# Weight splits between the steps of a pair's chain, and bias blocks in every second group, in a two-layer decoder trunk

## The chip, the cores and the metric

The kernel runs on one core of a Trainium2 chip. The time is the device time of one execution in microseconds; the kernel before takes 565.17 us (median of three runs, 564.53 to 566.84).

## What is computed

A trunk of two layers over 256 tokens with 1024 features, float32. Layer 0 mixes tokens by latent attention, layer 1 by block attention with a T5 bias; each is followed by an MLP with squared ReLU. The change touches the two MLPs alone.

```python
def sq_relu_mlp(h, w_in, w_out):        # w_in 1024 x 4096, w_out 4096 x 1024
    a = jax.nn.relu(h @ w_in)
    return (a * a) @ w_out

for i in range(DEPTH):                  # DEPTH = 2
    ...                                 # token mixer i, added to x
    h = rms_norm(x, mlp_norm[i])
    x = x + sq_relu_mlp(h, mlp_w_in[i], mlp_w_out[i])
```

In layer 1 each logit of the attention gets `rel_bias_table.T[h, t5_bucket(pos_q - pos_k)]` added. The kernel builds that bias (8 heads, 384 columns) during the MLP of layer 0.

## The kernel before

Everything is kept transposed: features on the 128 partitions, tokens along the row. To reach float32's accuracy with the fast matmul type, every operand is split into a high part (rounded) and a low part (the rest), and each product is three matmuls: high x high, low x high, high x low (`mm3`, 256 columns each). The row scale of the norm is not applied to h; it multiplies the result afterwards (`scale`).

**Weights** come in 185 units of 128 x 1024 numbers (512 KB), in the order of their use. SP's queue loads a unit into one of four `raw` buffers (`load_raw`), the scalar engine (ACT) rounds it into `wh` (`hi`, L169), the vector engine (DVE) subtracts to get `wl` (`lo`, L178). `wh` and `wl` have seven buffers each; `hi` does nothing when its unit is more than seven ahead of the last unit given as done (`done`). A raw buffer is free again after `lo`. `fill` (L181) does one low split, then one high split, so the low part of a unit is made a call later than its high part.

**The MLP** (`mlp`) has two halves r = 0, 1. In each half come eight *pairs* j (`first`): 256 columns of w_in, two units, 48 matmuls, and then a *chain* that makes `a`: relu (ACT, L922), square (DVE, L924), high part (ACT, L929), low part (DVE, L930). In layer 1's second half a multiplication by `scale` stands after the square. Then come eight *groups* d of w_out, two units and 48 matmuls each, numbered 8 to 15 behind the pairs; they read `a` of all eight pairs, the last pair's at the 43rd to 48th matmul. A group ends with y = psum x scale (DVE, L965) and x + y (POOL, L967). In the second half of layer 0 `finish0` goes on: x + y (POOL, L1030; DVE for the last), `make_h_filled` with hTh (ACT, L603), one `fill`, and hTl (DVE, L605), which is the input of layer 1's projections; after every second group ACT squares x for the next norm (L293) and POOL sums it (L295).

**The bias** is made in 12 blocks (`BiasBlock`), each in two places of layer 0's MLP. `steps`: the DVE compares positions, 128 x 1024, into `st` (L1006; two buffers). One place later `sums`: eight bf16 matmuls of 96 columns with `st` as weights, put into TensorE's row behind the 43rd matmul of the pair or group; and `add`: six DVE additions (L1023). `run_fillers` calls `steps` and `add` of a place. After matmuls of another type the first matmul of the next pair or group is made 258 columns wide (`wider`, L103).

Each engine works through its own instructions in the order in which the code issues them; the order of the lines in `mlp` is the order on the engines.

Of the kernel before, what the change touches and what calls it, by code (L numbers as in the profile page):

```python
# [25 lines left out]
KD = D // P  # L26
# [34 lines left out]
def trunk(ctx: ExitStack, tc: tile.TileContext, A, out):  # L61
# [119 lines left out]
    def fill(n=1):  # L181
        lo(n)
        hi(n)

    def unit(i):
        while len(his) <= i:
# [705 lines left out]
    def mlp(l, base, fillers, inside, finish):  # L892

        with tc.tile_pool(name=f"mlp{l}", bufs=1) as pool:
# [10 lines left out]
            def first(b, r, j, split_k, between=None):  # L905
                u = [unit(b + 2 * j + i) for i in range(2)]
                p = [ps() for _ in range(2 if split_k else 1)]
                o = [p[f][:, :S] if split_k else p[0][:, f * S:(f + 1) * S] for f in range(2)]
                for f, k in [(f, k) for k in range(KD) for f in range(2)] if split_k else \
                        [(f, k) for f in range(2) for k in range(KD)]:  # L910
                    c = (k % 4) * 256 + f * P
                    wide = None
                    if k == f == 0 and not moved[0]:
                        wide = wider(p[f], hTh)
                    mm3(o[f], part(u[k // 4], slice(c, c + P)), hT(k), k == 0, k == KD - 1, wide,
                        between if (f, k) == (1, KD - 2) else None)
                fill(2)
                run_fillers(r, j)
                for f, n in ((0, 1), (1, 1)) if split_k else ((0, 2),):
                    src = o[f] if split_k else p[0]  # L920
                    rl = t2(n * S)
                    nc.scalar.activation(rl, src, AF.Relu)  # L922
                    sq = t2(n * S)
                    nc.vector.scalar_tensor_tensor(sq, src, 0.0, rl, op0=OP.max, op1=OP.mult)  # L924
                    if l == 1 and r == NR - 1:
                        sq3 = sq.rearrange("p (a b) -> p a b", b=S)
                        nc.vector.tensor_mul(sq3, sq3, scale[:, None, :].to_broadcast([P, n, S]))
                    ah, al = (i[:, 2 * j + f:2 * j + f + n].rearrange("p a b -> p (a b)") for i in a)
                    nc.scalar.copy(ah, sq)  # L929
                    nc.vector.tensor_sub(al, sq, f32(ah))  # L930
                done(b + 2 * j + 1)

            for r in range(NR):
                b = base + r * (2 * NPAIR + 2 * KD)
                for j in range(NPAIR):
                    between = inside.get((r, j))
                    if r == 0 and j == 6:
                        pb = ps()
                        between = other_type(1, lambda: mm(pb[:, :S], ones, s, True, True))
                    first(b, r, j, r == 0 and j == 0, between)  # L940
                    if r == 0 and 1 <= j < 5:
                        sums.add(j - 1)
                    if r == 0 and j == 5:
                        s = sums.total()
                    if r == 0 and j == NPAIR - 1:
                        nc.vector.tensor_scalar(scale, pb[:, :S], 1.0 / D, EPS, op0=OP.mult, op1=OP.add)
                        nc.vector.reciprocal(scale, scale)
                b += 2 * NPAIR
                for d in range(KD):
                    bank = ps()  # L950
                    o = bank[:, :S]
                    for f in range(2 * NPAIR):
                        u = unit(b + 2 * d + f // 8)
                        c = (f % 8) * P
                        mm3(o, part(u, slice(c, c + P)), (a[0][:, f], a[1][:, f]), f == 0, f == 2 * NPAIR - 1,
                            wider(bank, a[0]) if f == 0 and not moved[0] else None,
                            inside.get((r, NPAIR + d)) if f == 2 * NPAIR - 2 else None)
                        if f == 7:
                            fill()
                            done(b + 2 * d)  # L960
                    fill()
                    run_fillers(r, NPAIR + d)
                    if l == 0 or r < NR - 1:
                        y = t2(S)
                        nc.vector.tensor_tensor(y, o, scale, op=OP.mult)  # L965
                        if r < NR - 1:
                            nc.gpsimd.tensor_add(x[:, d], y, x[:, d])  # L967
                            o = None
                        else:
                            o = y  # L970
                    if o is not None:
                        finish(d, o)
                    done(b + 2 * d + 1)
# [69 lines left out]
    inside = {}  # L1043
    fillers = [((0, 1), table_loads), ((0, 5), bias_tables)]
    for i, b in enumerate(blocks):
        r, j = (0, NPAIR + i) if i < KD else (1, (1, 4, 8, 10)[i - KD])
        place = (r, j + 1) if j + 1 < 2 * NPAIR else (r + 1, 0)
        fillers += [((r, j), b.steps), (place, b.add)]
        inside[place] = other_type(0, b.sums)
# [154 lines left out]
```

## Time and profile before

| | us |
|---|---|
| median of three runs | 565.17 |
| the profiled execution | 564.64 |
| its span | 562.5 |
| TensorE busy | 556.4 (99%) |
| DVE busy | 407.4 (72%) |
| ACT busy | 307.1 (55%) |
| POOL busy | 108.6 (19%) |

The page gives each engine's busy time. A timeline gives an engine's instructions with their start, and the idle time before them with what ended it; instructions of one kind in a row are one line with a count, whose time is from the first start to the last end. Ends of matmuls are modelled, and they overlap, so the pace of TensorE is read from starts, or from how many of them a stretch holds. PEld is its weight load. A wait can show there as a few tenths of a microsecond between starts.

### The profile page before, as it was taken

The numbers are of one execution on the slowest core, as the hardware profiler recorded it, in microseconds if no ns is written. First come the engines' busy times: TensorE is split into PE (matmuls) and PEld (weight loads), VectorE is DVE, ScalarE is ACT, GpSimd is POOL, SyncE is SP. The second block draws the span as 40 slices with busy tenths as digits, with TensorE's granted clock in tenths as the row PEclk, the third lists the DMA queues.
The fourth block names the chain that finished last, engine by engine and source line by source line (L and its number), as shares of the span: only waits on it lengthen the run. The fifth ranks groups of instructions, "written<-read, shape, count | busy, mean of one in ns | idle before, by whom it ended". The sixth has DMA issues, their size and how long they took to land.

```text
span 562.5 us, 10755 instructions
## 1 busy us (share of the span) xinstructions
PE 556.4 (99%) x4346; PEld 530.0 (94%) x4346; DVE 407.4 (72%) x654; ACT 307.1 (55%) x495; POOL 108.6 (19%) x105
## 2 busy tenths in 40 slices
PE   8999999999999999999999999999999999999997
PEld 6878999999999999999988888999999999999997
DVE  5997778587999987786658466777787665777641
ACT  5989676665343455543555465747655533555420
POOL 4892100041132200024324100000140232000100
PEclk9999999999999999999999999999999999999999
DMA  8833445655556656575665554444465766455830
GB/s 302 291 125 114 149 130 169 188 167 182 176 167 188 182 158 215 168 231 184 212 188 152 193 177 128 137 150 153 152 185 178 257 193 196 150 180 195 258 127 29
DMA packets 29185, 99.56 MB, mean 177 GB/s; under 512 B 3824, under 2 KB 4720, under 8 KB 29136
## 3 DMA queue, kind: packets, MB, share of 16 engines
q1 hardware_dynamic: 28656, 97.94, 54.4%
q0 software_dynamic: 336, 0.92, 0.4%
q8 instruction: 34, 0.56, 0.4%
q14 instruction: 15, 0.12, 0.1%
q10 hardware_dynamic: 144, 0.02, 0.0%
HBM read 97.82 MB, written 1.05 MB: 176 GB/s over the span
## 4 chain that ended last, share of the span: by engine, by line
PE 96%; DMA 2%; SPq 1%; issue 0%; DVE 0%; ACT 0%
PE ps L85 93%; PE ps L366 1%; DMA xs<-in_x_tok 1%; DMA win<-in_w_in 1%; PE ps L590 1%; SPq L158 0%; SPq L224 0%; PE ps L506 0%; DVE wl L178 0%; ACT wh L169 0%; DVE t L1039 0%; ACT sqj L471 0%; PE ps L873 0%
## 5 line engine op out<-in xcount | busy, mean ns | idle before, releaser
L169 ACT CAST wh<-raw 128x1024 fp32r<-128x1024 f32 x177 | 183.6, 1048 | 111.6 <-DMA raw<-in_w_out_mlp 56.6
L178 DVE TENSOR_TENSOR wl<-raw,wh 128x1024 fp32r<-128x1024 f32 x177 | 226.6, 1308 | 8.9 <-ACT wh L169 8.5
L85 PE MATMUL ps<-a,wh 128*128 128x256 f32 x1024 | 178.8, 278 | 0.0
L85 PEld LDWEIGHTS ps<-a,wh 128*128 128x128 f32 x1024 | 155.5, 188 | 0.4 <-DVE a L930 0.4
L85 PE MATMUL ps<-a,wl 128*128 128x256 f32 x512 | 142.9, 279 | 0.0
L85 PE MATMUL ps<-hTl,wh 128*128 128x256 f32 x512 | 141.9, 277 | 0.0
L85 PE MATMUL ps<-hTh,wl 128*128 128x256 f32 x512 | 141.8, 277 | 0.0
L85 PE MATMUL ps<-hTh,wh 128*128 128x256 f32 (+1 forms) x512 | 141.5, 276 | 0.0
L85 PEld LDWEIGHTS ps<-a,wl 128*128 128x128 f32 x512 | 96.2, 188 | 0.0
L85 PEld LDWEIGHTS ps<-hTh,wh 128*128 128x128 f32 x512 | 96.1, 188 | 0.1
L85 PEld LDWEIGHTS ps<-hTl,wh 128*128 128x128 f32 x512 | 96.1, 188 | 0.1
L85 PEld LDWEIGHTS ps<-hTh,wl 128*128 128x128 f32 x512 | 96.1, 188 | 0.0
L85 PE MATMUL ps<-aT,wh 128*128 128x256 f32 (+1 forms) x256 | 50.4, 288 | 0.0
L85 PE MATMUL ps<-wh,hTh 128*128 128x512 f32 (+2 forms) x128 | 46.2, 386 | 1.7 <-DVE wh L440 1.1
L85 PE MATMUL ps<-wl,hTh 128*128 128x512 f32 (+2 forms) x128 | 45.2, 378 | 0.1
L85 PE MATMUL ps<-wh,hTl 128*128 128x512 f32 (+2 forms) x128 | 44.8, 377 | 0.0
L967 POOL TENSOR_TENSOR x<-t,x 128x256 f32<-128x256 f32 x16 | 25.5, 1594 | 93.1 <-DVE t L965 93.1
L929 ACT CAST a<-t 128x512 fp32r<-128x512 f32 (+1 forms) x34 | 20.2, 596 | 38.3 <-DVE t L924 26.2
L85 PEld LDWEIGHTS ps<-aT,wh 128*128 128x128 f32 x256 | 40.3, 188 | 0.2
L924 DVE SCALAR_TENSOR_TENSOR t<-ps,t 128x512 f32<-128x512 f32 (+1 forms) x34 | 22.4, 658 | 24.1 <-ACT t L922 24.0
L930 DVE TENSOR_TENSOR a<-t,a 128x512 fp32r<-128x512 f32 (+1 forms) x34 | 22.5, 661 | 22.5 <-ACT a L929 22.5
L264 POOL TENSOR_TENSOR hrs<-hss,mhalf 128x4 f32<-128x4 f32 (+1 forms) x18 | 23.2, 1298 | 65.4 <-DVE hss L341 48.8
(166 smaller groups left out, 643.3 us busy)
## 6 DMA issues: line engine op xcount, KB each, us to landing
raw<-in_w_in_mlp SPq DMA_DIRECT2D x64, 512.0 KB, 4.0
raw<-in_w_out_mlp SPq DMA_DIRECT2D x64, 512.0 KB, 4.4
raw<-in_w_qkv SPq DMA_DIRECT2D x24, 512.0 KB, 4.4
raw<-in_w_u SPq DMA_DIRECT2D x8, 512.0 KB, 6.1
win<-in_w_in SPq DMA_DIRECT2D x8, 352.0 KB, 5.3
raw<-in_w_o0a SPq DMA_DIRECT2D x4, 512.0 KB, 3.9
raw<-in_w_o0b SPq DMA_DIRECT2D x4, 512.0 KB, 3.5
raw<-in_w_o1a SPq DMA_DIRECT2D x4, 512.0 KB, 4.1
```

What stands on the lines that cost most here:

```text
L85: nc.tensor.matmul(o, a, b, start=start, stop=stop)
L169: (eng.copy if eng is nc.scalar else eng.tensor_copy)(his[i][:, :w], raws[i][:, :w])
L178: eng.tensor_sub(los[i][:, :w], raws[i][:, :w], f32(his[i][:, :w]))
L264: nc.gpsimd.tensor_tensor(dst, t, mhalf[:, :n].rearrange("p (a b) -> p a b", b=t.shape[-1]) if len(t.shape) == 3 else mhalf[:, :n], op=OP.pow)
L366: nc.tensor.transpose(pt[:, i * P:(i + 1) * P], yf[:, i * P:(i + 1) * P], ident)
L590: nc.tensor.transpose(pt[:, i * P:(i + 1) * P], self.p[:, i * P:(i + 1) * P], ident)
L924: nc.vector.scalar_tensor_tensor(sq, src, 0.0, rl, op0=OP.max, op1=OP.mult)
L929: nc.scalar.copy(ah, sq)
L930: nc.vector.tensor_sub(al, sq, f32(ah))
L967: nc.gpsimd.tensor_add(x[:, d], y, x[:, d])
```

## The change

A new helper `both` makes a unit's high part and its low part right behind it. In `first`, `done` for the pair's two units comes ahead of the chain. `fill(2)` and `run_fillers` ahead of the chain are gone. For all pairs but the first of a layer and the last of each half (`beside`), one `both` stands between square and high part of `a`; after the chain come one more `both` (two for the pairs that have none inside), a further one for pairs 1 to 3, and then `run_fillers`. The groups use `both` where they used `fill`; `make_h_filled` keeps its `fill`. The steps of bias blocks 0 to 3 are put in groups 8, 10, 12, 14 of the first half, and those of blocks 4 to 11 in pairs and groups 0, 2, ... 14 of the second half; `sums` and `add` follow one place later. Before, blocks 0 to 7 had groups 8 to 15 of the first half, and the last four had pairs 1 and 4 and groups 8 and 10 of the second.

```diff
@@ -181,6 +181,12 @@
     def fill(n=1):
         lo(n)
         hi(n)
+
+    def both(n=1):
+
+        for _ in range(n):
+            hi()
+            lo()
 
     def unit(i):
         while len(his) <= i:
@@ -914,8 +920,10 @@
                         wide = wider(p[f], hTh)
                     mm3(o[f], part(u[k // 4], slice(c, c + P)), hT(k), k == 0, k == KD - 1, wide,
                         between if (f, k) == (1, KD - 2) else None)
-                fill(2)
-                run_fillers(r, j)
+                done(b + 2 * j + 1)
+
+
+                beside = not split_k and j < NPAIR - 1
                 for f, n in ((0, 1), (1, 1)) if split_k else ((0, 2),):
                     src = o[f] if split_k else p[0]
                     rl = t2(n * S)
@@ -925,10 +933,13 @@
                     if l == 1 and r == NR - 1:
                         sq3 = sq.rearrange("p (a b) -> p a b", b=S)
                         nc.vector.tensor_mul(sq3, sq3, scale[:, None, :].to_broadcast([P, n, S]))
+                    if beside:
+                        both()
                     ah, al = (i[:, 2 * j + f:2 * j + f + n].rearrange("p a b -> p (a b)") for i in a)
                     nc.scalar.copy(ah, sq)
                     nc.vector.tensor_sub(al, sq, f32(ah))
-                done(b + 2 * j + 1)
+                both((1 if beside else 2) + (1 <= j < 4))
+                run_fillers(r, j)
 
             for r in range(NR):
                 b = base + r * (2 * NPAIR + 2 * KD)
@@ -956,9 +967,9 @@
                             wider(bank, a[0]) if f == 0 and not moved[0] else None,
                             inside.get((r, NPAIR + d)) if f == 2 * NPAIR - 2 else None)
                         if f == 7:
-                            fill()
+                            both()
                             done(b + 2 * d)
-                    fill()
+                    both()
                     run_fillers(r, NPAIR + d)
                     if l == 0 or r < NR - 1:
                         y = t2(S)
@@ -1043,7 +1054,7 @@
     inside = {}
     fillers = [((0, 1), table_loads), ((0, 5), bias_tables)]
     for i, b in enumerate(blocks):
-        r, j = (0, NPAIR + i) if i < KD else (1, (1, 4, 8, 10)[i - KD])
+        r, j = (0, NPAIR + 2 * i) if i < 4 else (1, 2 * (i - 4))
         place = (r, j + 1) if j + 1 < 2 * NPAIR else (r + 1, 0)
         fillers += [((r, j), b.steps), (place, b.add)]
         inside[place] = other_type(0, b.sums)
```

How this moves instructions is seen in the engines' rows. `t` is a work buffer, `a_1321` and `a_1322` the high and low parts of `a`. First the DVE at the start of layer 0's second half. Before, from the square of pair 0 (`t_2608`) to that of pair 1 (`t_2677`):

```order
L924 SCALAR_TENSOR_TENSOR t_2608<-ps,t_2606 128x512
L930 TENSOR_TENSOR a_1322<-t_2608,a_1321 128x512
L178 TENSOR_TENSOR wl<-raw,wh 128x1024 x2
L1006 TENSOR_TENSOR st<-steps_q,steps_k 128x1024
L924 SCALAR_TENSOR_TENSOR t_2677<-ps,t_2675 128x512
L930 TENSOR_TENSOR a_1322<-t_2677,a_1321 128x512
```

After, from the square of pair 0 (`t_2538`) to that of pair 1 (`t_2617`):

```order
L932 SCALAR_TENSOR_TENSOR t_2538<-ps,t_2536 128x512
L178 TENSOR_TENSOR wl<-raw,wh 128x1024
L940 TENSOR_TENSOR a_1322<-t_2538,a_1321 128x512
L178 TENSOR_TENSOR wl<-raw,wh 128x1024
L1017 TENSOR_TENSOR st<-steps_q,steps_k 128x1024
L932 SCALAR_TENSOR_TENSOR t_2617<-ps,t_2615 128x512
L178 TENSOR_TENSOR wl<-raw,wh 128x1024
```

The two splits before `st` belonged to pair 1 and came ahead of its chain, and `st` was that of pair 1's place; now two splits and `st` of pair 0's place are behind the steps of pair 0's own chain.

ACT at the same place, before, from the relu of pair 0 to that of pair 1:

```order
L922 ACTIVATE t_2606<-ps 128x512
L929 CAST a_1321<-t_2608 128x512
L169 CAST wh<-raw 128x1024 x2
L922 ACTIVATE t_2675<-ps 128x512
L929 CAST a_1321<-t_2677 128x512
```

After:

```order
L930 ACTIVATE t_2536<-ps 128x512
L169 CAST wh<-raw 128x1024
L939 CAST a_1321<-t_2538 128x512
L169 CAST wh<-raw 128x1024
L930 ACTIVATE t_2615<-ps 128x512
```

A high split that stood behind the high part of `a` now stands ahead of it.

The DVE in the groups of layer 0's second half. Before, from y of group 9 (`t_3269`) to y of group 10 (`t_3343`):

```order
L965 TENSOR_TENSOR t_3269<-ps,scale 128x256
L178 TENSOR_TENSOR wl<-raw,wh 128x1024
L605 SCALAR_TENSOR_TENSOR hTl<-x,gains,hTh 128x256
L178 TENSOR_TENSOR wl<-raw,wh 128x1024 x2
L1006 TENSOR_TENSOR st<-steps_q,steps_k 128x1024
L965 TENSOR_TENSOR t_3343<-ps,scale 128x256
```

After, from y of group 9 (`t_3241`) to y of group 10 (`t_3311`):

```order
L976 TENSOR_TENSOR t_3241<-ps,scale 128x256
L611 SCALAR_TENSOR_TENSOR hTl<-x,gains,hTh 128x256
L178 TENSOR_TENSOR wl<-raw,wh 128x1024 x2
L1017 TENSOR_TENSOR st<-steps_q,steps_k 128x1024
L976 TENSOR_TENSOR t_3311<-ps,scale 128x256
```

No split is left between y and hTl. On ACT the two high splits of a group stand between hTh of one group and hTh of the next, before and after.

## Rows read from the trace of the kernel before

**Rows 1.** Page, parts 1 and 4: busy time and share; the chain by engine.

```profile
PE 556.4 (99%) x4346; PEld 530.0 (94%) x4346; DVE 407.4 (72%) x654; ACT 307.1 (55%) x495; POOL 108.6 (19%) x105
...
PE 96%; DMA 2%; SPq 1%; issue 0%; DVE 0%; ACT 0%
```

**Rows 2.** Stretches: us, then each engine's busy us (instructions), granted clock, DMA.

```profile
132.00:276.00 144.00, 144.00 (x1297) 143.10 (x1296) 120.29 (x181) 67.19 (x80) 25.32 (x16) 1.00 0.59 187
...
422.00:519.00 97.00, 97.00 (x858) 97.00 (x857) 67.37 (x73) 47.71 (x56) 12.30 (x8) 1.00 0.60 193
519.00:559.00 40.00, 40.00 (x342) 40.00 (x340) 17.72 (x20) 11.05 (x11) 4.03 (x7) 1.00 0.45 148
```

**Rows 3.** TensorE's timeline: start, us, engine, operation, count, idle time and its releaser.

```profile
143.04 0.30 PEld L85 LDWEIGHTS ps<-a,wh 128*128 128x128 f32 x2 [0.18 <-DVE a L930]
...
519.02 0.45 PE L85 MATMUL ps<-a,wh 128*128 128x256 f32 x2
519.31 0.28 PE L85 MATMUL ps<-a,wl 128*128 128x256 f32 x1
```

**Rows 4.** TensorE's timeline at a bias block: eight short matmuls, then the next.

```profile
201.88 0.52 PE L85 MATMUL ps<-parts,st 128*128 128x96 bf16 x8
...
202.42 0.28 PE L85 MATMUL ps<-hTl,wh 128*128 128x256 f32 x1
```

**Rows 5.** Timelines of TensorE, ACT, DVE: one pair's chain in layer 1.

```profile
393.89 0.28 PE L85 MATMUL ps<-hTh,wh 128*128 128x256 f32 x1
...
394.09 0.60 ACT L922 ACTIVATE t<-ps 128x512 f32<-128x512 f32 x1 [1.36 <-PE ps L85]
395.45 0.62 ACT L929 CAST a<-t 128x512 fp32r<-128x512 f32 x1 [0.76 <-DVE t L924]
...
394.72 0.69 DVE L924 SCALAR_TENSOR_TENSOR t<-ps,t 128x512 f32<-128x512 f32 x1 [2.30 <-ACT t L922]
396.10 0.69 DVE L930 TENSOR_TENSOR a<-t,a 128x512 fp32r<-128x512 f32 x1 [0.69 <-ACT a L929]
```

**Rows 6.** DVE's timeline, w_out groups of layer 0's second half.

```profile
249.60 2.36 DVE L178 TENSOR_TENSOR wl<-raw,wh 128x1024 fp32r<-128x1024 f32 x2
251.87 1.22 DVE L1006 TENSOR_TENSOR st<-steps_q,steps_k 128x1024 bf16<-128x1024 f32 x1
253.01 0.41 DVE L965 TENSOR_TENSOR t<-ps,scale 128x256 f32<-128x256 f32 x1
253.34 1.21 DVE L178 TENSOR_TENSOR wl<-raw,wh 128x1024 fp32r<-128x1024 f32 x1
255.73 0.48 DVE L605 SCALAR_TENSOR_TENSOR hTl<-x,gains,hTh 128x256 fp32r<-128x256 f32 x1 [1.18 <-ACT hTh L603]
256.67 1.23 DVE L178 TENSOR_TENSOR wl<-raw,wh 128x1024 fp32r<-128x1024 f32 x1 [0.45 <-ACT wh L169]
257.82 0.28 DVE L1023 TENSOR_TENSOR bias<-ps,mask 128x128 f32<-128x128 f32 x1
...
259.52 0.41 DVE L965 TENSOR_TENSOR t<-ps,scale 128x256 f32<-128x256 f32 x1
```

**Rows 7.** POOL's and ACT's timelines, same stretch: x + y, hTh, the high splits.

```profile
253.57 1.59 POOL L1030 TENSOR_TENSOR x<-t,x 128x256 f32<-128x256 f32 x1 [4.95 <-DVE t L965]
...
255.19 0.51 ACT L603 ACTIVATE hTh<-x,gains 128x256 fp32r<-128x256 f32 x1 [3.61 <-POOL x L1030]
255.61 1.99 ACT L169 CAST wh<-raw 128x1024 fp32r<-128x1024 f32 x2
```

**Rows 8.** ACT's, POOL's and DVE's timelines in a group with the norm's square.

```profile
262.10 0.62 ACT L293 ACTIVATE t<-x 128x512 f32<-128x512 f32 x1
...
262.80 1.30 POOL L295 TENSOR_TENSOR ssum<-t,t 128x512 f32<-128x512 f32 x1 [1.14 <-ACT t L293]
...
263.69 1.48 DVE L178 TENSOR_TENSOR wl<-raw,wh 128x1024 fp32r<-128x1024 f32 x1 [0.98 <-ACT wh L169]
```

**Rows 9.** DVE's timeline, the reciprocal ahead of layer 0's first w_out group.

```profile
143.36 1.75 DVE L947 RECIPROCAL scale<-scale 128x256 f32<-128x256 f32 x1
```

## The prediction

> **What bounds the kernel now.** I read the page first: TensorE is busy for 99% of the span, and the chain that ended last is 96% TensorE [rows 1]. So only two things move the end: how fast TensorE takes its matmuls, and how long it waits between them. Next the stretches. In 422 to 519 us it takes 858 matmuls in 97.0 us, 0.1132 us each; in 519 to 559 it takes 342 in 40.0 us, 0.1178 us each, at the same granted clock of 1.00 (the upper level, 2.4 GHz) [rows 2]. There are two paces, and the slow one costs 4%. The rows around the change of pace show what starts it: from 519.02 to 519.31 two matmuls take 0.29 us instead of 0.23 [rows 3]. That is the end of the first w_out group of layer 1's second half, where the last pair's `a` is read. At the same place in layer 0, at 143.04, a weight load has waited for the DVE's `a` [rows 3]. In this kernel a short wait of TensorE is therefore paid twice: once itself, and then by the slow pace until a widened matmul (258 columns, `wider`) comes, if one comes.
>
> How much is that in all? 132 to 276 us holds 1297 matmuls, 96 of them the short ones of the bias blocks. A block costs TensorE 0.43 us: from 201.88 to 202.42 is 0.54, with one long matmul of 0.11 in it [rows 4]. 144.0 - 1199 x 0.1132 - 12 x 0.43 leaves 3.1 us; about 0.3 of it is the six slow matmuls around each block, which stay. In 519 to 559 it is 40.0 - 340 x 0.1132 = 1.5 us. So **all waits and all slow pace in the two MLPs are worth 2.8 + 1.5 = 4.3 us**. That is the most the change can win there: 564.64 us (the profiled execution; span 562.5; the median of the three is 565.17) would become 560.3.
>
> **The change, part by part.**
>
> *Last pair's chain first* (relu, square, high, low, then the splits). After a pair's last matmul (next pair begins at 393.89) the relu starts 0.20 later, the square 0.83, the low part of `a` 2.2, ending at 2.9 [rows 5]. TensorE needs it at the 43rd matmul of the next group, 43 x 0.1132 = 4.87 us. This wait goes, in both layers: here the 1.5 us of layer 1 and the slow stretch behind 143.04 are won. In layer 1 nothing else is moved onto TensorE's path, since it has no bias blocks and its last add needs no `hT`.
>
> *High and low split together, between the chain's steps.* No instruction is added. Low parts come right behind high parts, six units ahead of their use; the wait at a late low part goes with the rest of the 4.3. But the chain gets longer: relu to 0.80, high split to 1.8 (two take 1.99 on ACT [rows 7]), low split 1.8 to 3.0, low part of `a` to 3.6, second low split 3.55 to 4.75. For `a` itself that does no harm, it is read much later.
>
> *The bias steps behind that chain.* This does harm. `run_fillers` moves from ahead of the chain to behind it. Before, `st` of a pair stood in the DVE's row ahead of the pair's square and needed nothing of that pair. Now it stands behind square, low split, low part, low split (front: the DVE's rows), so it cannot start before 4.7 us after the pair's end, and takes 1.22 [rows 6]: it ends at 5.9. TensorE wants it at the 43rd matmul of the next pair, 4.87 us after, and its queue stands still until then. That is a wait of 1.05 us, four times (blocks 4 to 7, in pairs 1, 3, 5, 7 of the second half). Behind pair 1 a third split (1.14) and the adds (1.70 [rows 6]) keep the DVE until 7.5 us after that pair's end, which is 2.1 after the end of pair 2; so pair 2's chain starts late, and the wait in pair 3 is 0.9 longer. Sum: 4 x 1.05 + 0.9 = **5.1 us**.
>
> *The w_out groups of the second half of layer 0.* Here the splits meet a loop. Each group ends with y (DVE), x + y (POOL), hTh (ACT), hTl (DVE). Before, the DVE had a low split whose high part was long done, and did it between y and hTl (253.34 in [rows 6]). Now every high part has its low part at once, so nothing is left: the high splits stand behind hTh on ACT, and both low splits behind hTl on the DVE (front). From the rows: y starts at 253.01, POOL's x + y runs to 255.16, the high splits behind hTh start at 255.61 [rows 6, 7], and the first low split that waits for it starts at 256.67, **3.66 us after y** [rows 6]. In every second group ACT's square for the norm stands ahead too: 259.52 to 263.69 is 4.17, and the split then lasts 1.48 beside POOL's sum instead of 1.22 [rows 6, 8]. The second low split takes 1.14 of the DVE's time more, as the first does (two: 2.36, and 2.27 until the next instruction). Then come adds, 1.70 (257.82 to 259.52), or `st`, 1.14 until the next instruction [rows 6], then the next y. So y to y is 3.66 + 2.28 + 1.70 = 7.64 and 4.17 + 0.3 + 2.28 + 1.14 = 7.89: **15.5 us for two groups, where TensorE needs 2 x 48 x 0.1132 + 0.43 = 11.3**. The DVE falls behind by 4.2 us in two groups, and it is `st`, which stands in this loop, that hands the lateness to TensorE.
>
> Where does it begin? Group 8 starts as pair 7 ends. The DVE's row is chain to 2.9, two low splits to 5.5 (the first waits for its high part, 3.2), adds to 7.2, low split 8.4, `st` 9.5, then y(8), which is 4.0 after group 9 starts at 5.44. Block 8 is wanted at 10.3: in time by 0.8. From group 9's start: y(9) at 11.65, `st` of block 9 ends at 19.6; group 11 starts at 11.3 and wants it at 16.2. **Wait 3.4 us, then 4.2 and 4.2** at blocks 10 and 11 (groups 13 and 15): 11.8 us. y(15) is then 6.5 us into the projections, and hTl of the last row 8.4, wanted after 42 matmuls of 512 columns. Those take over 9.6 us at twice 0.1132 each, so nothing more waits.
>
> *Blocks in every second group elsewhere.* In groups 8 to 15 of the first half there is no hT loop. The DVE has 2.3 of splits, 0.3 of y and 1.1 or 1.7 of bias work in 5.4 to 5.9 us: it keeps up. The first `st` (group 8) is close: chain to 2.9, splits behind their high parts to 5.5, scale and reciprocal 2.1 (an estimate: 1.75 of it is the reciprocal [rows 9]), split, `st` to about 10.0, wanted at 10.3. The bound is 0 to 1 us, and I take 0.
>
> *Slow pace that stays.* Behind a block the pace comes back only if the widened matmul restores it. From group 9 of the first half to group 9 of the second there are some 90 us: 0 if always, 3.3 us if never (90 x 4% less what stays anyway). I take 0.8, since the rows of before show long fast stretches behind blocks. In the groups where TensorE waits for the DVE, its pace costs nothing.
>
> **Sum:** 564.64 - 4.3 + 0.8 + 5.1 + 11.8 = **578.1 us**, 2.4% longer.
>
> **The rivals.**
>
> *Everything in time.* `st` is done before TensorE asks, as it is now at 201.88 [rows 4]. For it speaks that the DVE now has a block in each of eight groups in a row, of which half is left there, and that it is busy in only 407 of 562 us [rows 1]. Against it speaks that the new waits come from latency, not load. It decides at 4.87 us after a pair's end (the chain must lose 1.0) and at 11.3 us for two groups (the loop must lose 4.2). Time: 564.64 - 4.3 + 0.8 = 561.1 at most, 560.3 at best. That is faster. Chance 0.08.
>
> *Only the pairs wait*, because the loop of the groups starts earlier than I reckon or its second low split fits beside POOL: 561.1 + 5.1 = 566.2, the same within 0.5%. Chance 0.05.
>
> *Only the groups wait*, the steps of the pairs being covered: 561.1 + 11.8 = 572.9. Chance 0.07.
>
> *The clock falls in the waits.* All rows here are at granted 1.00, and TensorE never stands for 3 us inside the MLPs, so nothing in the trace shows what a wait of 4 us does. If the next group ran at half pace, the first two times it would be swallowed (TensorE has 4.2 us to spare there), the third time it would cost up to 48 x 0.1132 = 5.4 us: 578.1 to 583.5. Chance 0.10. The Trainium skill, "TensorE: Matmul & The Clock Gate", part 1, "What's actually happening", says that an idle array is taken back to the throttled clock of 1.2 GHz and that activity releases it; by that rule this rival is what happens if the wait is long enough, and no run here shows such a wait.
>
> **How the numbers follow.** Forecast 578, chance 0.70; its own ends are 0 and 3.3 for the pace, 0 to 1 for the first block, and half a microsecond either way in each of seven waits: 573 to 583. The range takes in the groups alone (572.9) and the fallen clock (583): 571 to 583; outside lie the pairs alone, all in time, and some 0.05 of the forecast. A measurement of this kernel tells 0.5% (2.8 us) from no change. Slower by more: 0.70 + 0.07 + 0.10 = 0.87. Same: 0.05. Faster: 0.08.
>
> **What would show it.** In the changed trace, TensorE's weight loads of `st` wait for the DVE: about 1 us in pairs 1, 5, 7 and 2 us in pair 3 of layer 0's second half, and 3 to 4 us in its groups 11, 13 and 15, none in group 9. The DVE idles over 2 us between y and hTl in those groups, and y to y takes 7.6 to 7.9 us. Layer 1 runs at 0.1132 us to the end, 1.5 us shorter. The prediction is wrong if `st` ends ahead of its weight load in those places, if low splits still stand between y and hTl, or if the low part of the last pair's `a` is still waited for.

## The result, and the profile after

| | before | after |
|---|---|---|
| median | 564.69 us | 572.34 us |
| lowest to highest (six each) | 563.54 to 566.84 | 572.02 to 573.90 |
| the profiled execution, its span | 564.64, 562.5 | 572.02, 570.2 |
| ratio of the times, 95% interval | | 1.014, 1.0117 to 1.0163 |

The change makes the kernel 7.7 us slower, 1.4%; the forecast was 578, 13.4 us slower, in a range of 571 to 583. The direction, the seven places and the cause of the waits came out; one term of the sum, the waits in the groups, was more than twice too large. The page of the kernel after shows it first, in the parts that answer to [rows 1]: busy time and share of each engine, then the chain that ended last, by engine and by line.

```profile
PE 556.4 (98%) x4346; PEld 529.7 (93%) x4346; DVE 396.1 (69%) x654; ACT 302.6 (53%) x495; POOL 93.8 (16%) x105
...
PE 86%; DVE 7%; issue 3%; ACT 2%; POOL 1%; DMA 1%; SPq 0%; ACTq 0%; POOLq 0%
PE ps L85 83%; DVE wl L178 3%; ACT wh L169 2%; DVE st L1017 2%; PE ps L372 1%; DVE bias L1034 1%; PE ps L596 1%; POOL x L1041 1%; DMA win<-in_w_in 1%; DVE a L940 0%; DVE t L976 0%; ACT t L299 0%; PE ps L512 0%; DVE t L932 0%; DVE t L1050 0%
```

TensorE's share of the chain falls from 96% to 86%, and the 7% of the DVE are the instructions of the two new chains: low splits (`wl`), `st`, adds (`bias`), with ACT's high splits and POOL's x + y between them. The DVE is less busy than before (396.1 us after 407.4), and so is POOL (93.8 after 108.6). The loss is latency, not load.

Now the waits. These are the weight loads of `st` that waited, in the order of time; at the end of a row stands the idle time of the load and what ended it.

```profile
194.66 0.37 PEld L85 LDWEIGHTS <-st 128*128 128x128 bf16 x8 [1.08 <-DVE st L1017]
207.90 0.37 PEld L85 LDWEIGHTS <-st 128*128 128x128 bf16 x8 [1.55 <-DVE st L1017]
220.35 0.24 PEld L85 LDWEIGHTS <-st 128*128 128x128 bf16 x5 [1.14 <-DVE st L1017]
232.73 0.33 PEld L85 LDWEIGHTS <-st 128*128 128x128 bf16 x7 [1.08 <-DVE st L1017]
...
256.84 0.24 PEld L85 LDWEIGHTS <-st 128*128 128x128 bf16 x5 [1.07 <-DVE st L1017]
270.64 0.37 PEld L85 LDWEIGHTS <-st 128*128 128x128 bf16 x8 [2.11 <-DVE st L1017]
284.51 0.24 PEld L85 LDWEIGHTS <-st 128*128 128x128 bf16 x5 [2.19 <-DVE st L1017]
```

Four stand in pairs 1, 3, 5, 7 of layer 0's second half (4.9 us, forecast 5.1), three in groups 11, 13, 15 (5.4 us, forecast 11.8). Group 9 does not wait, as forecast. How a pair's wait comes about is in the DVE's timeline for the end of pair 0:

```profile
189.58 0.69 DVE L932 SCALAR_TENSOR_TENSOR t<-ps,t 128x512 f32<-128x512 f32 x1 [4.79 <-ACT t L930]
190.51 1.23 DVE L178 TENSOR_TENSOR wl<-raw,wh 128x1024 fp32r<-128x1024 f32 x1 [0.24 <-ACT wh L169]
191.66 0.68 DVE L940 TENSOR_TENSOR a<-t,a 128x512 fp32r<-128x512 f32 x1
192.26 1.22 DVE L178 TENSOR_TENSOR wl<-raw,wh 128x1024 fp32r<-128x1024 f32 x1
193.39 1.22 DVE L1017 TENSOR_TENSOR st<-steps_q,steps_k 128x1024 bf16<-128x1024 f32 x1
```

Square, low split, low part of `a`, low split, and only then `st`, which ends at 194.61; the load follows at 194.66. Ahead of the square the DVE stood idle for 4.79 us: it had all the time that `st` needs, but `st` was behind the chain in its row. In the groups this is the DVE's row from one y (L976) to the next but one, with POOL's x + y of the same stretch and ACT's work behind it:

```profile
243.15 0.42 DVE L976 TENSOR_TENSOR t<-ps,scale 128x256 f32<-128x256 f32 x1
245.03 0.48 DVE L611 SCALAR_TENSOR_TENSOR hTl<-x,gains,hTh 128x256 fp32r<-128x256 f32 x1 [1.46 <-ACT hTh L609]
245.97 2.36 DVE L178 TENSOR_TENSOR wl<-raw,wh 128x1024 fp32r<-128x1024 f32 x2 [0.46 <-ACT wh L169]
...
249.95 0.41 DVE L976 TENSOR_TENSOR t<-ps,scale 128x256 f32<-128x256 f32 x1
251.82 0.48 DVE L611 SCALAR_TENSOR_TENSOR hTl<-x,gains,hTh 128x256 fp32r<-128x256 f32 x1 [1.46 <-ACT hTh L609]
253.29 2.36 DVE L178 TENSOR_TENSOR wl<-raw,wh 128x1024 fp32r<-128x1024 f32 x2 [0.98 <-ACT wh L169]
255.56 1.22 DVE L1017 TENSOR_TENSOR st<-steps_q,steps_k 128x1024 bf16<-128x1024 f32 x1
256.70 0.42 DVE L976 TENSOR_TENSOR t<-ps,scale 128x256 f32<-128x256 f32 x1
...
243.71 0.74 POOL L1041 TENSOR_TENSOR x<-t,x 128x256 f32<-128x256 f32 x1 [58.10 <-DVE t L976]
...
244.48 0.51 ACT L609 ACTIVATE hTh<-x,gains 128x256 fp32r<-128x256 f32 x1 [5.71 <-POOL x L1041]
244.90 1.98 ACT L169 CAST wh<-raw 128x1024 fp32r<-128x1024 f32 x2
```

The order is the one that was forecast: nothing between y and hTl, both low splits behind hTl, adds or `st` behind those. But y to y is 6.80 and 6.75 us, not 7.64 and 7.89, because POOL's x + y takes 0.74 us, where it took 1.59 in [rows 7]. (From the next group on it is 6.79 and then 7.02 or 7.08: there POOL's sum for the norm runs too, and a low split beside it lasts 1.49 or 1.56.)

What the change wins is there too. The stretches that answer to [rows 2], with TensorE's busy time, matmuls and granted clock (the first two are layer 1's MLP):

```profile
431.00:527.00 96.00, 96.00 (x849) 1.00 0.63 193
527.00:566.50 39.50, 39.50 (x351) 1.00 0.36 118
...
183.53:193.50 9.97, 9.97 (x90) 1.00 0.25 62
257.97:268.45 10.48, 10.48 (x91) 1.00 0.40 140
```

Layer 1 goes at 0.113 us a matmul to its end: the 1.5 us of [rows 2] are won, and no weight load waits for the last pair's `a` any more, as one did in [rows 3]. The last two rows show the two paces in layer 0: two matmuls that reach into each stretch aside, 88 take 9.97 us (0.1133) ahead of the first wait, 89 take 10.48 (0.1178) between the waits of blocks 9 and 10, at the same granted clock. By the starts of the matmuls four such stretches stayed slow (behind blocks 4, 7, 9, 10), 353 matmuls, 1.6 us.

So the sum with measured terms: 564.64 - 4.3 + 1.6 + 4.9 + 5.4 = 572.2, where 572.02 was measured.

### The profile page after: what moved, and what is told of

Read it like the earlier page. It is cut to its first block, busy times and chain, and to the rows that moved or that the text cites. A ratio compares the mean times of both kernels' runs of the same rounds, so it can differ in the third digit from the quotient of the medians.

```text
span 570.2 us, 10793 instructions
## 1 busy us (share of the span) xinstructions
PE 556.4 (98%) x4346; PEld 529.7 (93%) x4346; DVE 396.1 (69%) x654; ACT 302.6 (53%) x495; POOL 93.8 (16%) x105
## 3 DMA queue, kind: packets, MB, share of 16 engines
HBM read 97.82 MB, written 1.05 MB: 173 GB/s over the span
## 4 chain that ended last, share of the span: by engine, by line
PE 86%; DVE 7%; issue 3%; ACT 2%; POOL 1%; DMA 1%; SPq 0%; ACTq 0%; POOLq 0%
PE ps L85 83%; DVE wl L178 3%; ACT wh L169 2%; DVE st L1017 2%; PE ps L372 1%; DVE bias L1034 1%; PE ps L596 1%; POOL x L1041 1%; DMA win<-in_w_in 1%; DVE a L940 0%; DVE t L976 0%; ACT t L299 0%; PE ps L512 0%; DVE t L932 0%; DVE t L1050 0%
## 5 line engine op out<-in xcount | busy, mean ns | idle before, releaser
L178 DVE TENSOR_TENSOR wl<-raw,wh 128x1024 fp32r<-128x1024 f32 x177 | 216.7, 1239 | 39.0 <-ACT wh L169 38.4
L85 PE MATMUL ps<-a,wh 128*128 128x256 f32 x1024 | 176.5, 277 | 0.0
L85 PE MATMUL ps<-hTh,wh 128*128 128x256 f32 x512 | 141.4, 276 | 0.0
L930 ACT ACTIVATE t<-ps 128x512 f32<-128x512 f32 (+1 forms) x34 | 19.4, 571 | 71.9 <-PE ps L85 71.9
L609 ACT ACTIVATE hTh<-x,gains 128x256 fp32r<-128x256 f32 x24 | 12.2, 510 | 49.1 <-POOL x L1041 30.9
L85 PE MATMUL ps<-aT,wl 128*128 128x256 f32 x128 | 35.6, 278 | 0.0
L978 POOL TENSOR_TENSOR x<-t,x 128x256 f32<-128x256 f32 x16 | 20.3, 1269 | 92.5 <-DVE t L976 92.5
```

The lines of the kernel that those rows point to most:

```text
L85: nc.tensor.matmul(o, a, b, start=start, stop=stop)
L178: eng.tensor_sub(los[i][:, :w], raws[i][:, :w], f32(his[i][:, :w]))
L609: nc.scalar.activation(hTh[:, k], x[:, k], AF.Copy, scale=gain(gname, k))
```

## The experiments

"Theory" is the prediction's: TensorE waits because `st` stands late in two chains. The first question is whether the seven waits have these two causes and nothing else; the second why the groups' term was too large; the third what each part of the change does alone. Times are medians; ratios are to the kernel before, on the same chip.

### A pair's bias work ahead of its chain again

```diff
                 done(b + 2 * j + 1)
+                run_fillers(r, j)
...
                 both((1 if beside else 2) + (1 <= j < 4))
-                run_fillers(r, j)
```

> The changed kernel, but with the bias work of a pair (st and adds) put ahead of the pair's chain again. Latency theory: TensorE waits in pairs 1, 3, 5, 7 only because st stands behind the chain and its splits; the four waits (4.7 us) vanish, the three in groups 11, 13, 15 (5.3 us) stay: 572.3 - 4.7 = 567.6 us. Load theory (the DVE has too much to do in the second half with a block in every second place, wherever the instructions stand): the lateness comes back as waits of the chain or at other blocks, 571 us or more.

565.6 us, ratio 1.0024 (1.0008 to 1.0041). The four waits in the pairs are gone: `st` of blocks 5 to 7 is done 3.3 to 4.4 us before its load, with the same work on the DVE. That ends the load theory for the pairs. The result is 2 us better than the latency theory said. The DVE also comes to the groups earlier, and two of their waits are left, 3.1 us (weight loads of `st`, idle time and times); and with the pairs' waits most of the slow stretches are gone (the table below). In the profiled execution the granted clock fell as well, behind block 10's wait of 2.5 us.

```profile
  DVE st L1016: 3.1, 2
```

### The old splits in the groups of the second half

```diff
                         if f == 7:
-                            both()
+                            (fill if l == 0 and r == NR - 1 else both)()
...
-                    both()
+                    (fill if l == 0 and r == NR - 1 else both)()
```

> The changed kernel, but the groups of layer 0's second half split as before: a low part one call behind its high part. Loop theory: a low split stands between y and hTl again, the loop from y to the next y falls below TensorE's 11.3 us for two groups, though POOL's x + y beside that low split goes back from 0.74 to about 1.6 us; the three waits in groups 11, 13, 15 (5.3 us) vanish and the four in the pairs (4.7 us) stay: 572.3 - 5.3 = 567.0 us. Load theory: at least half of the three waits stays, 570 us or more.

568.96 us, ratio 1.0076 (1.0051 to 1.01). A miss for both: of 5.4 us in the groups 2.8 stay, half of it as the load theory said, but the time is below its 570. The DVE's row over one group shows why:

```profile
248.65 0.41 DVE L976 TENSOR_TENSOR t<-ps,scale 128x256 f32<-128x256 f32 x1
248.98 1.22 DVE L178 TENSOR_TENSOR wl<-raw,wh 128x1024 fp32r<-128x1024 f32 x1
251.37 0.48 DVE L611 SCALAR_TENSOR_TENSOR hTl<-x,gains,hTh 128x256 fp32r<-128x256 f32 x1 [1.17 <-ACT hTh L609]
252.84 1.23 DVE L178 TENSOR_TENSOR wl<-raw,wh 128x1024 fp32r<-128x1024 f32 x1 [0.98 <-ACT wh L169]
253.98 1.22 DVE L1017 TENSOR_TENSOR st<-steps_q,steps_k 128x1024 bf16<-128x1024 f32 x1
255.11 0.42 DVE L976 TENSOR_TENSOR t<-ps,scale 128x256 f32<-128x256 f32 x1
```

A low split does stand between y and hTl again, but POOL's x + y beside it takes 1.58 us, so hTl comes 2.72 us after y, where it came 1.88 after y in the changed kernel. What is won on one side (one low split, 1.14) is mostly lost on the other (0.84). y to y is 6.46 here, some 13 us for two groups: still over TensorE's 11.3. The old splits alone do not make room for a block in every second group.

### Both edits

> Both edits at once: bias work of a pair ahead of its chain, and the splits of the second half's groups as before. If the two causes are the whole loss: 572.3 - 4.7 - 5.3 = 562.3 us, and if the slow pace behind blocks that had a wait (some 350 matmuls of 4.5 ns more, 1.6 us) goes with the waits, 560.7. That is 2 to 4 us under the kernel before. Rival (placing a block in eight places in a row costs something by itself): 564.7 us or more.

562.77 us, ratio 0.997 (0.9956 to 0.9985): 0.3% faster than the kernel before. The rival falls. What was left was read from one more run of the same kernel:

> The version with the pairs' bias work first and the old splits in the late groups once more, for its trace: 562.8 us as measured. From 560.3 us without any wait some 2.5 are left; if they are waits for st, they stand in groups 13 and 15 (about 1 us each).

562.56 us. Two waits for `st`, in groups 13 and 15, 1.8 us together (0.2 and 1.6, not one each), and one slow stretch of 87 matmuls behind the first.

### The steps one place earlier

```diff
-        fillers += [((r, j), b.steps), (place, b.add)]
+        fillers += [((r, j - 1) if j else (r - 1, 2 * NPAIR - 1), b.steps), (place, b.add)]
```

> The changed kernel with its splits as they are, but each block's steps issued one pair or group earlier (sums and adds where they were). If TensorE loses time through st alone: all seven waits vanish though the loop of the groups stays at 6.8 us from y to y, 562.3 us (560.7 if the slow pace goes too). If the loop itself holds TensorE up (late hTl, a low split that comes late for its group, the adds' banks): new waits of 2 us or more in the groups or at the first projections, 565 us or more.

565.34 us, ratio 1.0008 (0.9989 to 1.0028). The second case of the expectation, in one part: the waits for `st` are gone but for 0.5 us, and at the end of layer 0 a new one stands in the first projections (TensorE's weight loads):

```profile
287.60 0.19 PEld L85 LDWEIGHTS ps<-wh,hTh 128*128 128x128 f32 x1 [3.45 <-ACT hTh L609]
288.12 0.19 PEld L85 LDWEIGHTS ps<-wh,hTl 128*128 128x128 f32 x1 [0.33 <-DVE hTl L611]
```

In the pairs nothing is handed on: there `st` only stood in the wrong place, and 4.9 us are won. In the groups the loop itself is too long; when `st` no longer passes its lateness to TensorE, the last row of h does. The prediction had said that nothing more waits there. That holds only while TensorE is held up in the groups.

### The POOL instruction that came out at half its length

Two kernels with one added DVE instruction of equal length in seven groups, between y and hTl, whose result is not used: a subtraction of two tensors, and a maximum of one.

```diff
         eng.tensor_add(x[:, d], o, x[:, d])
+        if d < KD - 1:
+            nc.vector.tensor_sub(spare, flat(f32(a_now[0][:, :4])), flat(f32(a_now[1][:, :4])))
```

> The changed kernel with one more DVE instruction in seven groups of layer 0's second half, between y and hTl, where the DVE stands idle for about 1.4 us: a subtraction of two SBUF operands, 128 x 1024, about 1.2 us, whose result nobody reads. Theory (x + y on POOL took 1.59 us before because a DVE instruction with two SBUF inputs ran beside it, and 0.74 alone): x + y goes from 0.74 to about 1.6, the loop from y to y from 6.8 to about 7.6 us, the waits in groups 11, 13, 15 from 5.3 to between 9 and 12: 576 to 579 us, which is the forecast that was made for the changed kernel. Rival (x + y is short for another reason, its operands or its place): x + y stays at 0.74 and the time at 572 to 573.

> The same as the run with a two-input subtraction beside x + y, but the added DVE instruction is a maximum along the row: one SBUF operand, 128 x 1024, one number per row written. Theory (only a second SBUF input of the DVE stands in POOL's way): x + y stays at about 0.74, the loop at 6.8 us, the time at 572 to 573. Rival (any DVE work beside it does): x + y about 1.6, the time 576 or more.

577.78 us, ratio 1.0219 (1.0187 to 1.0252), and 571.41, ratio 1.0112 (1.009 to 1.0134). The DVE's and POOL's rows of one group, first with two operands, then with one:

```profile
251.32 0.41 DVE L980 TENSOR_TENSOR t<-ps,scale 128x256 f32<-128x256 f32 x1
251.65 1.22 DVE L1048 TENSOR_TENSOR spare<-a,a 128x1024 f32<-128x1024 f32 x1
...
251.88 1.59 POOL L1046 TENSOR_TENSOR x<-t,x 128x256 f32<-128x256 f32 x1 [6.05 <-DVE t L980]
```

```profile
249.42 0.41 DVE L980 TENSOR_TENSOR t<-ps,scale 128x256 f32<-128x256 f32 x1
249.75 1.21 DVE L1048 TENSOR_REDUCE spare<-a 128x1 f32<-128x1024 f32 x1
...
249.98 0.74 POOL L1046 TENSOR_TENSOR x<-t,x 128x256 f32<-128x256 f32 x1 [6.05 <-DVE t L980]
```

The DVE is equally busy in both, 1.22 and 1.21 us at the same place. Beside the two-operand instruction x + y takes 1.59 us, beside the one-operand one 0.74, and so in all seven groups (medians 1.584 and 0.738). That is the mis-sized term, shown: with x + y at 1.59 the loop takes 7.63 us from y to y (the forecast said 7.64), the waits for `st` rise from 10.2 to 13.6 us (16.9 were forecast), and the time to the 578 that was forecast. The Trainium skill, "SBUF — State Buffer", section "Who interferes with whom", states this as a rule: a DVE instruction with two inputs in SBUF contends with a GpSimd (POOL) instruction that reads SBUF, and one with at most one input there, outside the modes that use two ports, does not. The two runs agree with it; the price here is 0.85 us on 0.74.

The two added instructions differ in one thing more: the subtraction writes 128 x 1024 numbers, the maximum one column. That the write is the cause is unlikely by two rows of the changed kernel. A POOL addition of the same size keeps 0.75 us beside the square, which writes 128 x 512 but reads only one operand from SBUF (the other, `ps`, is in psum):

```profile
127.12 0.75 POOL L306 TENSOR_TENSOR ssum<-ssum 128x256 f32<-128x256 f32 x1
127.44 0.69 DVE L932 SCALAR_TENSOR_TENSOR t<-ps,t 128x512 f32<-128x512 f32 x1 [1.54 <-ACT t L930]
```

POOL began first there, and second in the two runs, so this is not the same case in everything.

The time of the first of the two holds something else, though: the clock. Stretches of it with TensorE's busy time, matmuls and granted clock, behind the wait for block 9 and behind the one for block 11:

```profile
259.00:261.00 2.00, 1.94 (x16) 0.65 1.00 371
261.00:263.00 2.00, 2.00 (x11) 0.50 0.06 21
263.00:266.00 3.00, 3.00 (x27) 1.00 0.33 85
...
290.00:292.00 2.00, 1.90 (x14) 0.58 0.91 352
292.00:293.60 1.60, 1.60 (x5) 0.50 0.18 74
```

After waits of 2.8 and 3.9 us, and not after the one of 2.3 between them, TensorE was granted the lower level (1.2 GHz) for some 3.4 us; its matmuls of 256 columns took 0.213 us instead of 0.113, which cost 1.7 and 1.5 us. In the middle of the groups such a fall is swallowed. The one-operand run had one behind block 10's wait of 2.1 us, and its next wait was 0.6 us where the changed kernel's was 2.2. Behind the last block it is paid. So 577.78 is nearer to the forecast than its mechanism alone earns, by about 1.5 us. In the trace of the kernel after, no wait did this, also not the 2.11 us at 270.64:

```profile
270.60:272.60 2.00, 1.96 (x22) 1.00 0.96 363
```

### Each part of the change alone

The blocks alone, in the kernel before:

```diff
-        r, j = (0, NPAIR + i) if i < KD else (1, (1, 4, 8, 10)[i - KD])
+        r, j = (0, NPAIR + 2 * i) if i < 4 else (1, 2 * (i - 4))
```

> The kernel before with only the bias blocks moved to the changed kernel's places; splits, chains and the pairs' steps as before. In the run with the old splits in the groups the loop from y to y took 13.0 to 13.2 us for two groups with a block, over TensorE's 11.3. Theory A (the new places do harm of their own in the second half's groups, through that loop): waits of 1.2 and 1.6 us in groups 13 and 15, less the slow pace of about 2 us that the places take from the first half: 564 to 565.5 us. Theory B (the places are harmless, only the splits and steps wait): no wait over 0.3 us, 562.5 us. In both the last pair's a is still waited for in both layers.

564.88 us, ratio 0.9991 (0.9976 to 1.0007). Theory A: waits for `st` of 0.5 and 1.6 us in groups 13 and 15. Some 150 matmuls fewer at the slow pace (0.7 us) stand against them, and the time cannot be told from that of the kernel before.

The splits and the chain alone, with the blocks where they were:

> The changed kernel with the bias blocks at their old places (groups 8 to 15 of the first half; pairs 1 and 4 and groups 8 and 10 of the second half). Theory: harm needs splits and places together. Two waits of about 1.05 us in the pairs (blocks 8, 9), about 1.0 in group 11 (block 11), none in groups 13 and 15; 1.5 us won in layer 1 and 0.3 in the waits for a; up to 1 us of slow pace: 564.6 - 1.8 + 3.1 + 0 to 1 = 566 to 567 us. Rival (the splits alone make the loss): 571 us or more.

566.19 us, ratio 1.0011 (0.9987 to 1.0035). Two waits in the pairs, 3.4 us, and none in the groups (block 11 is in time by 0.3). The first is 2.2 us and not 1.05: the last adds of the first half now stand behind pair 0's chain too, and make pair 1's late. The profiled execution took 563.1 us. Its ten executions fall into two sets by the mean granted clock: 563.1 to 564.5 us at 0.999 to 1.0 (four), 566.1 to 567.6 at 0.997 (six). The profiled one is of the first set; that the clock falls behind the waits in the second is likely by this, but no trace of one was taken.

So neither part alone can be told from no change in time, though each has waits of its own (2.1 and 3.4 us) that its gains cover; together they cost 1.4%: the splits lengthen the loop of the groups and put `st` behind the chains, the new places put twice as many `st` there.

The last pair's chain alone, in the kernel before:

```diff
-                fill(2)
-                run_fillers(r, j)
+                if j < NPAIR - 1:
+                    fill(2)
+                    run_fillers(r, j)
...
+                if j == NPAIR - 1:
+                    fill(2)
+                    run_fillers(r, j)
                 done(b + 2 * j + 1)
```

> The kernel before with one thing changed: after the last pair of each half the chain comes ahead of the two splits. Theory: the last pair's a is no longer waited for; layer 1 keeps the fast pace to its end (1.5 us) and the waits of 0.15 us at its place in each half go: 565.0 - 1.5 to 2.5 = 562.5 to 563.5 us. Rival (the slow pace in layer 1 has another cause): 564.5 to 565.

573.04 us, ratio 1.0139 (1.0111 to 1.0166): a miss on both sides. The wait for `a` is gone, and in its place stands a longer one for a low split, once in each half of both layers, 6.1 us in all. This is the first (weight load):

```profile
142.52 0.19 PEld L85 LDWEIGHTS ps<-a,wl 128*128 128x128 f32 x1 [1.25 <-DVE wl L178]
```

With low parts made one call behind their high parts, the split that was put behind the chain is one that the group needs 24 matmuls after its start. In the changed kernel two low splits stand at the same place (141.17, 2.36 us) and nobody waits, because there low parts come right behind high parts and are further ahead of their use. The 1.5 us of layer 1 are not won by the chain's place alone; the run with splits and chain wins them. The new order of the splits without the chain's place was not run.

### A version that beats both kernels

```diff
                 done(b + 2 * j + 1)
+                run_fillers(r, j)
...
-                run_fillers(r, j)
...
-                            both()
+                            (fill if l == 0 and r == NR - 1 else both)()
...
-                    both()
+                    (fill if l == 0 and r == NR - 1 else both)()
...
-        r, j = (0, NPAIR + 2 * i) if i < 4 else (1, 2 * (i - 4))
+        r, j = (0, (8, 10, 11, 13, 14, 15)[i]) if i < 6 else (1, (1, 3, 5, 7, 9, 11)[i - 6])
```

> A version built from the findings: the changed kernel with a pair's bias work ahead of its chain, the old splits in the groups of layer 0's second half, and the blocks moved out of that half's late groups: groups 8, 10, 11, 13, 14, 15 of the first half, pairs 1, 3, 5, 7 and groups 9, 11 of the second. Theory: the loop of those groups no longer has a block in every second group, no st is waited for, nothing is left to start the slow pace: 560.3 to 561.5 us. Rival (three blocks close together in the first half, or the four in the pairs, overload the DVE): waits of 1 us or more there, 563 us or more.

560.23 us, ratio 0.992 (0.99 to 0.994): 0.8% faster than the kernel before, by the medians 2.1% faster than the changed one, and the 560.3 that the prediction gave for "all waits and all slow pace gone". Its page and its MLP of layer 0:

```profile
PE 552.3 (99%) x4346; PEld 526.5 (94%) x4346; DVE 398.4 (71%) x654; ACT 303.1 (54%) x495; POOL 99.5 (18%) x105
...
132.00:276.00 144.00, 144.00 (x1309) 1.00 0.58 183
```

No `st` is waited for (the closest is in time by 0.4 us, in the first group), and the same 144 us hold 1309 matmuls, where [rows 2] had 1297. Then the same with the changed kernel's splits in the late groups:

> The same as the version with the blocks out of the late groups, but with the changed kernel's splits in those groups, low part right behind high part. If splits and blocks harm only together: two groups of the loop take 13.6 us less 2.8 for st and adds, 10.8, under TensorE's 11.3, so again no wait: 560.3 to 561.5 us. If the splits' order alone makes the loop too long: waits in the groups or at the first projections, 563 us or more.

561.41 us, ratio 0.9943 (0.992 to 0.9966). One wait of 0.7 us, in group 12 for the block of group 11, and a slow stretch behind it. Without a block in every second group the loop keeps up also with those splits, nearly.

### The parts of every trace, added up

The floor is 560.3 us. To it come the waits of TensorE (idle time of its weight loads before `st`, `a`, a low split or the first projections), the 256-column matmuls that started 117 to 121 ns apart, counted from 100 us on and beyond the 176 that the best version also has, at 4.6 ns each, and 1.6 us for each fall of the clock.

| profiled execution of | waits | slow matmuls more | clock | sum | measured |
|---|---|---|---|---|---|
| before | 0.4 | 784 | 0 | 564.3 | 564.6 |
| after | 10.2 | 345 | 0 | 572.1 | 572.0 |
| pairs' bias work first | 3.1 | 53 | 1 | 565.2 | 564.7 |
| old splits in the groups | 7.7 | 240 | 0 | 569.1 | 569.3 |
| both (second run) | 1.8 | 86 | 0 | 562.5 | 562.6 |
| steps one place earlier | 4.3 | 0 | 0 | 564.6 | 564.7 |
| two operands beside | 13.6 | 411 | 2 | 579.0 | 579.2 |
| one operand beside | 8.7 | 335 | 1 | 572.1 | 571.5 |
| splits alone | 3.4 | 0 | 0 | 563.7 | 563.1 |
| blocks alone | 2.1 | 632 | 0 | 565.3 | 565.3 |
| chain alone | 6.1 | 1267 | 0 | 572.2 | 573.3 |
| best version, new splits in the late groups | 0.7 | 144 | 0 | 561.7 | 562.0 |
| best version | 0 | 0 | 0 | 560.3 | 560.2 |

With these three prices every run comes out to within 0.6 us, the one with the chain alone to within 1.1.

## Why the prediction was right, and where it was off

**The time**: inside the range of 571 to 583, and partly by luck. The forecast's own ends were 573 to 583, and 572.3 lies below them; the range reached down to 571 for the rival "only the groups wait" (572.9), which did not happen.

**What bounds the kernel, and the 4.3 us** to be won: right. The best version, which has neither waits nor slow stretches, took 560.2, and layer 1's 1.5 us came as forecast. The prediction put this gain down to the chain's place; the run with the chain alone shows that it needs the new order of the splits as well.

**The pairs**: right, 4.9 us for 5.1, in the four places, by the chain as told, and gone with the one edit that undoes it. The lateness handed on to pair 3 was sized too high: its wait is 1.55 us, where 1.95 was forecast.

**The groups**: right in mechanism and in place, wrong in size, 5.4 us for 11.8. The step that failed is "POOL's x + y runs to 255.16 ... 3.66 us after y": it took POOL's 1.59 us from a row where a low split with two operands ran beside it [rows 6, 7], and kept it for a loop from which the same paragraph had removed that split. From y to the first low split it is then 2.82 and 3.34 us, not 3.66 and 4.17; the rest of the loop with the adds, 3.98 us, came out to the hundredth. Two groups fall behind by 2.2 to 2.6 us, not by 4.2, and the three waits shrink accordingly. The signs that hang on this term failed with it: the DVE idles 1.46 us between y and hTl, not over 2, and y to y is 6.7 to 7.1 us, not 7.6 to 7.9. The right number stood in the trace of the kernel before, in layer 1, where one x + y ran while the DVE waited for its next split:

```profile
438.57 0.74 POOL L967 TENSOR_TENSOR x<-t,x 128x256 f32<-128x256 f32 x1 [2.12 <-DVE t L965]
439.38 2.49 DVE L178 TENSOR_TENSOR wl<-raw,wh 128x1024 fp32r<-128x1024 f32 x2 [0.88 <-ACT wh L169]
```

**The first group and the end**: the first `st` was in time by 0.4 (0.3 forecast), the one of group 9 by 1.2 (0.8 forecast). "Nothing more waits" at the projections held in the changed kernel, and not where the lateness was no longer taken by `st`. (Small slips of the working, without effect: 42 matmuls at twice 0.1132 are 9.5 us, not 9.6; 40.0 us over the 340 whole matmuls of [rows 2] are 0.1176 each; the five terms of the sum give 578.0, and the ends listed for the range 573.7 and 585.)

**Slow pace that stays**: 1.6 us for 0.8, inside the bounds of 0 and 3.3.

**The rivals.** "Everything in time", "only the pairs" and "only the groups" are out, by the seven waits. "The clock falls" did not happen in the profiled execution. The mean granted clock is 0.999 in three of the changed kernel's six executions (572.02, 572.17 and 572.50 us) and 0.996 or 0.997 in the other three (572.08, 573.90 and 573.73), as it is 0.997 in the one-operand run with its one fall; so a fall in those three is likely, but none of them was traced. Three experiments show it after waits of 2.1 to 3.9 us, swallowed or paid as the rival said, but for 1.5 to 1.7 us and not 5.4. The page that the prediction named for it (the Trainium skill, "TensorE: Matmul & The Clock Gate", "What's actually happening") says that an idle array falls back to 1.2 GHz; these traces agree, but a wait of 3.45 us in the run with the earlier steps passed without it, so its length alone does not tell.

## What to carry to other kernels

A duration from a trace belongs to what ran beside it: when an edit takes the neighbour away, look for a row of the same instruction without that neighbour before you carry the number over (here there was one, 0.74 us, in another layer). An instruction that needs nothing of a chain, but stands behind it in an engine's row, passes the chain's latency on to whoever waits for it, however idle the engine is; put it ahead of the chain. And two edits that each leave the time as it was, because their gains hide their waits, can cost 1.4% together when both burden the same loop, so sum the loop from one end to the other against the pace of the engine it feeds.

## What the runs showed of the hardware

The same POOL addition (128 x 256, float32) took 0.74 us alone or beside a one-operand DVE reduction and 1.57 to 1.64 beside a two-operand DVE subtraction.

TensorE's matmuls of 256 columns have two paces at the same granted clock of 1.00, 0.1133 and 0.1178 us, and a wait of a microsecond can leave it at the slower one for the next 87 to 89 matmuls, up to the next block. It does not always: behind block 5 with a wait of 1.55 us the changed kernel went on fast, and the same place in the run with the two-operand subtraction went on slow. What decides it stays open; no run here tells.

Waits of 2.11 us (changed kernel) and 3.45 us (steps one place earlier) left the granted clock at 1.00; a wait of 2.11 us in the run with one operand beside, for the same block, was followed by these two rows:

```profile
270.00:272.00 2.00, 1.89 (x15) 0.61 0.96 354
272.00:274.00 2.00, 2.00 (x12) 0.53 0.16 61
```

So the length alone does not decide it; what else does was not tried.
